# An attention kernel on one core: the first bias chunk is loaded behind q and k and added behind the scores

## The chip, the cores and the metric

The kernel runs on one core of one Trainium2 chip. The metric is device time in microseconds. Beside the times there is one profiled execution of the kernel before, with a trace of every instruction and of the DMA packets.

## The reference

Attention with a bias: 4 batches of 8 heads, 1024 positions, head dimension 64, all float32. The bias is one 1024 x 1024 matrix, shared by all heads.

```python
scale = 1.0 / np.sqrt(head_dim)
scores = scale * np.matmul(q, k.transpose(0, 1, 3, 2))
scores = scores + bias
scores_max = np.max(scores, axis=-1, keepdims=True)
attn = np.exp(scores - scores_max) / (np.sum(np.exp(scores - scores_max), axis=-1, keepdims=True) + 1e-8)
return np.matmul(attn, v).astype(np.float32)
```

## The kernel before

**Units of work.** The 32 heads form 16 pairs. The 1024 queries of a head form 8 chunks of 128 (query `p * 8 + c` is row `p` of chunk `c`). One slot is one head's chunk `c`: a 128 x 1024 block of scores, held transposed (keys down, queries across, in 8 pieces of 128 keys) in one of three places in PSUM (`places`, two banks each). A slot is filled by 8 score matmuls of 128 x 128 (L244), then ScalarE takes exp of it into a bfloat16 tile `E` (L258), and TensorE multiplies `E` with `v` and a column of ones (L312), so that the last column is the sum of the exps; VectorE divides (L320, L322) and SP stores. 19 of the 256 slots take their exp on VectorE by a polynomial instead.

**The bias is added once per place.** A run of slots in one place is made for the same chunk `c` and head after head. Only the first slot of a run (`start`, the fourth field in `slots`) gets the bias, by 8 matmuls of the bias with a scaled identity `ident8` (L241); the next slots add the difference of their scores and those of the head before to what lies in PSUM (the `ke`/`ko` and `qe`/`qo` arrays hold the pair's k and plus or minus q for that). The first three slots of the program are such starts: slot 0 is chunk 0 of head 0 in place 0, slot 1 chunk 1 in place 1, slot 2 chunk 2 in place 2. Each of the 8 bias matmuls of a slot takes every eighth column of the 1024 columns of `braw[:, c, :]`.

**Order of work.** The schedule is manual: the order in which the program issues instructions is the order on each engine. From slot 1's exp on it is made by a planner in the kernel, which keeps a model of the engines' times (`T0`, `bias_at`, `raw_at`, costs) and issues whatever its model has ready first. The planner's code and figures are the same in both kernels. What lies ahead of it, lines 335 to 392, is written out by hand, and that is what the change edits.

**The start, written out by hand.** Pair 0 is loaded in float32 by hardware queues: SP's queue takes `q0f` (the first `C0 = 3` chunks of q, 192 KB) and then `k0f` in two halves (256 KB each), ScalarE's queue takes `b0f`, bias chunk 0 (512 KB). GpSimd makes the identity, clears halves of `qz` and `qs` (two memsets, L350 and L351) and then issues the software loads, which cast to bfloat16 on the way: bias chunks 1 and 2, pair 1's k and q, pair 2's k and q, v of pair 0, and so on for the other pairs. TensorE meanwhile runs 10 matmuls of zeros (L360). Then: VectorE casts q and the first half of k (L370, L371); ScalarE casts the bias and then the second half of k (L372, L373); TensorE transposes q, k's first half and k's second half (L187, the last into PSUM place 2); VectorE copies them out to `qz`, `ko` and `qo` (L378, L199, L201). Slots 0 and 1 get their bias before their scores, and slot 0's exp is done in two halves, each as soon as half the keys' scores are there:

```python
for i in range(2):
    fill_half(0, i, "b")
transposes(0, 1, half, half, None, px=pk2)
copy_out(0, 1, half, half, pk2)
copy_out(0, 0, 0, C0, pq)
fill_half(0, 0, "s")
exp(0, 0, 1)
for i in range(2):
    fill_half(1, i, "b")
fill_half(0, 1, "s")
exp(0, 1, 1)
```

`fill(s)` then fills the rest of slot 1 (scores alone) and slot 2 (bias, then scores), and all slots after them.

Of the kernel before, what the change touches and what calls it, by code (L numbers as in the profile page):

```python
# [16 lines left out]
def kernel(  # L17
# [13 lines left out]
    nc = tc.nc  # L31
    B, H, S, D = q.shape
    P = 128
# [5 lines left out]
    qf = q.rearrange("b (g t) (p c) d -> (b g) p t (c d)", t=2, p=P)  # L39
    kf = k.rearrange("b (g t) (p c) d -> (b g) p t (c d)", t=2, p=P)  # L40
    vf = v.rearrange("b (g t) (p c) d -> (b g) p t c d", t=2, p=P)
    of = out.rearrange("b h (p c) d -> p (b h) c d", p=P)
    bf_ = bias.rearrange("a b (p c) k -> p (a b c) k", p=P)
# [9 lines left out]
    C0 = 3  # L53
# [22 lines left out]
    qs = consts.tile([P, NCH, P], BF)  # L76
    qz = [consts.tile([P, NCH, P], BF, name=f"qz{x}") for x in range(2)]
    zeros = ep.tile([P, NCH, P], BF, name="E")[:, :4].rearrange("p c q -> p (c q)")
    braw = consts.tile([P, NCH, S], BF)
# [4 lines left out]
    b0f = dp.tile([P, S], F32, name="df")  # L84
    q0f = dy.tile([P, S], I32, name="dy").bitcast(F32)[:, :2 * C0 * D].rearrange("p (t c d) -> p t c d", t=2, d=D)
    k0f = dp.tile([P, S], F32, name="dt").rearrange("p (t c d) -> p t c d", t=2, d=D)
    places = [ps_s.tile([P, 2, 512], F32, name=f"pl{x}") for x in range(3)]


    slots = []  # L90
# [72 lines left out]
    def load_v(pr):  # L163
        lands[pr, "v"] = vland.tile([P, 2, NCH, D], BF, name="v16")
        nc.gpsimd.dma_start(out=lands[pr, "v"].rearrange("p t c d -> p t (c d)"),  # L165
                            in_=vf[pr].rearrange("p t c d -> p t (c d)"))
        return lands[pr, "v"][:1, 1, NCH - 1, D - 1:]
# [14 lines left out]
    def transposes(pr, which, c0, n, tag, px=None):  # L182
        if px is None:
            px = ps_x.tile([P, n, P], BF, tag=tag, name="px")
        for c in range(n):
            if (pr, which, c0) in raws:
                nc.tensor.transpose(px[:, c, :], raws[pr, which, c0][:, c].rearrange("p t d -> p (t d)"), ident[:])  # L187
                continue

            for t in range(2):  # L190
                nc.tensor.transpose(px[t * D:(t + 1) * D, c, :], lands[pr, which, c0][:, t, c, :], ident[:],  # L191
                                    tile_position=(0, t * D))
        return px

    def copy_out(pr, which, c0, n, px):
        t = arrays(pr)
        cs = slice(c0, c0 + n)
        if which:
            nc.vector.tensor_copy(t["ko"][:, cs, :], px[:])  # L199
        else:  # L200
            nc.vector.tensor_scalar(t["qo"][:, cs, :], px[:], sgn[:], None, op0=ALU.mult)  # L201

    def double(pr, which, c0, n, part, w):

        t = arrays(pr)
        cs = slice(c0, c0 + n)
        rows = slice(D, P) if part == 1 else slice(0, D)
        to = arrays(pr + 1) if part == 1 else t
        if which:
            w.tensor_copy(to["ke"][rows, cs, :], t["ko"][rows, cs, :])  # L210
        else:
            w.tensor_scalar(to[("qe", "qe", "qs", "qz")[part]][rows, cs, :], t["qo"][rows, cs, :], -1.0, 1.0,
                            op0=ALU.mult, op1=ALU.mult)
# [11 lines left out]
    def operands(s):  # L225
        x, c, h, start = slots[s]
        pr = h // 2
        t = arrs[pr]
        if start:
            return t["ko"], t["qz"] if pr in first_pair else t["qs"]  # L230
        return (t["ko"], t["qo"]) if h % 2 else (t["ke"], t["qe"])

    def fill_half(s, b, what):

        x, c, h, start = slots[s]
        kk, qq = operands(s)
        for i in range(4):
            kc = 4 * b + i
            to = places[x][:, b, i * P:(i + 1) * P]
            if what == "b":  # L240
                nc.tensor.matmul(to, braw[:, c, :].rearrange("p (kp kc) -> p kc kp", kc=NCH)[:, kc, :], ident8[:],  # L241
                                 start=i == 0, stop=False, skip_group_check=True)
            else:
                nc.tensor.matmul(to, kk[:, kc, :], qq[:, c, :], start=False, stop=True, skip_group_check=True)  # L244

    def fill(s):
        for what in "bs" if slots[s][3] and s > 1 else "s":
            for b in range(2):
                fill_half(s, b, what)

    etile = {}

    def exp(s, i=0, n=2):

        if i == 0:
            etile[s] = ep.tile([P, NCH, P], BF, name="E")
        e = etile[s].rearrange("p (b c) q -> p b (c q)", b=2)
        nc.scalar.activation(e[:, i:i + n].rearrange("p b x -> p (b x)"),  # L258
                             places[slots[s][0]][:, i:i + n].rearrange("p b x -> p (b x)"), ACTF.Exp, scale=scale)
# [75 lines left out]
    with tc.manual_schedule():  # L335

        half = NCH // 2
        nc.sync.dma_start(out=q0f[:], in_=qf[0][:, :, :C0 * D].rearrange("p t (c d) -> p t c d", d=D))
        nc.scalar.dma_start(out=b0f[:], in_=bf_[:, 0, :])
        for i in range(2):  # L340
            nc.sync.dma_start(out=k0f[:, :, i * half:(i + 1) * half].rearrange("p t c d -> p t (c d)"),
                              in_=kf[0][:, :, i * half * D:(i + 1) * half * D])
        nc.vector.memset(zeros, 0.0)
        nc.vector.memset(warm[:], 0.0)
        nc.vector.memset(sgn[:D, :], -1.0)
# [2 lines left out]
        make_identity(nc, ident[:])  # L348

        nc.gpsimd.memset(qz[0][D:, :, :], 0.0)  # L350
        nc.gpsimd.memset(qs[D:, :, :], 0.0)  # L351
        for c in (1, 2):
            load_b(c)
        load_k(1)
# [1 line left out]
        load_k(2)  # L356
        load_q(2, slice(0, NCH))
        load_v(0)
        for i in range(10):
            nc.tensor.matmul(places[2][:, 0, :], zeros[:, :P], zeros, start=True, stop=True)  # L360

        cast = [de.tile([P, NCH, P], BF, name="de").rearrange("p c (t d) -> p c t d", d=D) for i in range(2)]
        qr0 = raws[0, 0, 0] = cast[0][:, half:half + C0]
# [5 lines left out]
        nc.vector.tensor_scalar(ident8[:], ident[:], 1.0 / scale, None, op0=ALU.mult)  # L369
        nc.vector.tensor_copy(qr0.rearrange("p c t d -> p t c d"), q0f[:])  # L370
        nc.vector.tensor_copy(kr0[0].rearrange("p c t d -> p t c d"), k0f[:, :, :half])  # L371
        nc.scalar.copy(braw[:, 0, :], b0f[:])  # L372
        nc.scalar.copy(kr0[1].rearrange("p c t d -> p t c d"), k0f[:, :, half:])  # L373

        pq = transposes(0, 0, 0, C0, "xa")
        pk = transposes(0, 1, 0, half, "xb")
        pk2 = places[2].bitcast(BF)[:, 1, :half * P].rearrange("p (c x) -> p c x", x=P)
        nc.vector.tensor_scalar(t0["qz"][:D, :C0, :], pq[:D], 1.0, None, op0=ALU.mult)  # L378
        copy_out(0, 1, 0, half, pk)
        for i in range(2):  # L380
            fill_half(0, i, "b")
        transposes(0, 1, half, half, None, px=pk2)
        copy_out(0, 1, half, half, pk2)
        copy_out(0, 0, 0, C0, pq)
        fill_half(0, 0, "s")
        exp(0, 0, 1)
        for i in range(2):
            fill_half(1, i, "b")
        fill_half(0, 1, "s")
        exp(0, 1, 1)  # L390
        double(0, 1, 0, NCH, 1, nc.vector)
        double(0, 0, 0, C0, 1, nc.vector)

# [363 lines left out]
        def dve_pick():  # L757

            can = [x for x in dve_q if (x[1] < 4 or len(dav) < 2) and (x[1] != 0.5 or len(open_d) < 3)]
            if not can:  # L760
                return None
            best = min(can, key=lambda x: (max(x[0], t_dve), x[1]))
            start = max(best[0], t_dve)

            if best[1] >= 3:
                soon = [x for x in can if x[1] < 3 and x[0] < start + 350]
                if soon:
                    best = min(soon, key=lambda x: (x[0], x[1]))
            return best
# [4 lines left out]
        while next_fill < NS or next_act < len(acts) or avq or dav or dve_q or sp_q:  # L774
            c = []
            if next_act < len(acts):

                s = min(x for x in acts[next_act:] if filled[x] <= max(t_act, filled[acts[next_act]]))
# [5 lines left out]
            d = dve_pick()  # L784
            if d:
                c.append((max(t_dve, d[0]), 1))
            p = pe_pick()
# [6 lines left out]
            if not c:  # L794
                p = min(pe_cands(), key=lambda x: x[0])
                c.append((p[0], 2))
            t, who = min(c)
            if who == 0:
                s = acts[next_act]
# [45 lines left out]
```

## Time and profile before

| | us |
|---|---|
| median of 3 runs (lowest, highest) | 233.12 (232.87, 233.36) |
| the profiled execution's own time | 233.77 |
| span of that profile, first to last instruction | 232.0 |
| PE busy in the span | 223.4 (96%) |
| ScalarE (ACT) busy | 221.5 (95%) |
| VectorE (DVE) busy | 196.8 (85%) |
| GpSimd (POOL) busy | 64.6 (28%) |

The difference of 1.8 us between the profiled execution's time and its span lies outside the instructions. In the lines of the profile, `L244 PE MATMUL pl<-qo,ko` is line, engine, operation and `out<-in` by the tiles' names. PE is the matmul side of TensorE and PEld its weight loads; SPq and ACTq are the DMA issues of SP and ScalarE. In the timeline, the first column is the start in the span and the second the duration, `xN` means that N instructions are merged into one line, and the bracket tells how long the engine was idle before it and what ended that. In the DMA view, q1 is SP's hardware queue, q10 ScalarE's, and q0 the software queue that GpSimd feeds. The granted clock of the profile is 1.00 in nearly the whole span.

### The profile page before, as it was taken

To read this page: it belongs to the slowest core of one execution; us is meant where nothing else is said; L and a number is where in the kernel's file an instruction comes from. 1 tells how busy PE (TensorE), PEld (TensorE's weight loads), DVE (VectorE), ACT (ScalarE), POOL (GpSimd) and SP (SyncE) were. 2 spreads that over 40 slices of the span, in tenths; PEclk is the share of its full clock that TensorE was granted. 3 is DMA by queue.
4 is the path that set the end of the run, shared out by engine and by line. 5 is a ranking of instruction groups with operands and counts; after the bars stand their busy time and mean duration, and the time that the engine had idled before them with its cause. 6 is when DMAs were issued, how large, how long until landed. Compare 5 with 4: busy or idle time off the path is not lost.

```text
span 232.0 us, 10693 instructions
## 1 busy us (share of the span) xinstructions
PE 223.4 (96%) x4671; PEld 210.0 (91%) x4671; DVE 196.8 (85%) x294; ACT 221.5 (95%) x242; POOL 64.6 (28%) x114
## 2 busy tenths in 40 slices
PE   7899999999999999999999999999999999999993
PEld 2779898899999999999999999999998999999992
DVE  2485768699988999799989789899999899999993
ACT  3699999999999999999999999999999999999994
POOL 8836653155553625325326210000000000000000
PEclk9999999999999999999999999999999999999999
DMA  6999999899999899998999965111111112112212
GB/s 200 210 205 225 215 226 223 185 114 120 168 189 142 126 192 151 123 173 155 191 206 197 237 114 128 43 37 40 42 37 49 39 48 57 54 29 71 68 38 62
DMA packets 55645, 29.75 MB, mean 128 GB/s; under 512 B 31856, under 2 KB 51952, under 8 KB 55600
## 3 DMA queue, kind: packets, MB, share of 16 engines
q0 software_dynamic: 30336, 14.06, 49.3%
q1 hardware_dynamic: 24832, 14.43, 22.4%
q8 instruction: 36, 0.59, 1.1%
q10 hardware_dynamic: 432, 0.59, 1.0%
q14 instruction: 9, 0.07, 0.1%
HBM read 29.36 MB, written 8.39 MB: 163 GB/s over the span
## 4 chain that ended last, share of the span: by engine, by line
ACT 25%; PE 15%; issue 11%; DMA 6%; DVE 6%; SPq 1%; DVEq 0%; ACTq 0%
ACT E L258 25%; PE pl L244 10%; PE po L312 4%; DMA out_dram<-ob 3%; DMA qe<-q 3%; SPq L694 1%; DVE ob L322 1%; DVE dt L290 1%; DVE dy L275 1%; DVE de L295 1%; PE px L191 1%; DVE df L280 1%; DVE df L287 0%; PE pl L241 0%; DVE rs L320 0%
## 5 line engine op out<-in xcount | busy, mean ns | idle before, releaser
L258 ACT ACTIVATE E<-pl 128x1024 bf16<-128x1024 f32 (+1 forms) x238 | 218.3, 1116 | 2.5 <-PE pl L244 2.1
L312 PE MATMUL po<-vall,E 128*128 128x65 bf16 x1896 | 92.0, 194 | 1.3 <-ACT E L258 0.7
L312 PEld LDWEIGHTS <-E 128*128 128x128 bf16 x1896 | 77.5, 98 | 2.4 <-ACT E L258 1.1
L244 PE MATMUL pl<-qo,ko 128*128 128x128 bf16 x1024 | 77.0, 219 | 1.0 <-ACT E L258 0.4
L244 PEld LDWEIGHTS <-ko 128*128 128x128 bf16 x1160 | 69.5, 98 | 4.1 <-issue 1.1
L244 PE MATMUL pl<-qe,ke 128*128 128x128 bf16 x888 | 66.3, 219 | 1.0 <-issue 0.3
L244 PEld LDWEIGHTS <-ke 128*128 128x128 bf16 x888 | 53.4, 98 | 3.9 <-issue 0.7
L275 DVE TENSOR_SCALAR dy<-pl 128x1024 int32<-128x1024 f32 x19 | 23.2, 1222 | 4.5 <-PE pl L244 3.7
L322 DVE TENSOR_TENSOR ob<-po,rs 128x448 f32<-128x448 f32 (+2 forms) x40 | 23.2, 581 | 3.4 <-DVE rs L320 1.1
L284 DVE SCALAR_TENSOR_TENSOR dt<-df 128x1024 f32<-128x1024 f32 x19 | 23.2, 1221 | 0.3
L295 DVE SCALAR_TENSOR_TENSOR de<-dy,dt 128x1024 uint16<-128x1024 int32 x19 | 23.2, 1219 | 0.1
L287 DVE SCALAR_TENSOR_TENSOR df<-dt,df 128x1024 f32<-128x1024 f32 x19 | 23.1, 1219 | 0.1
L290 DVE SCALAR_TENSOR_TENSOR dt<-df,dt 128x1024 f32<-128x1024 f32 x19 | 23.1, 1218 | 0.1
L138 POOL DMA_DIRECT2D q<-in_q_dram x18 | 16.7, 930 | 7.5 <-PE pl L244 6.1
L201 DVE TENSOR_SCALAR qo<-px,sgn 128x1024 bf16<-128x1024 bf16 (+2 forms) x18 | 12.4, 686 | 3.4 <-PE px L191 1.7
L199 DVE COPY ko<-px 128x1024 bf16<-128x1024 bf16 (+1 forms) x16 | 10.7, 671 | 4.4 <-PE px L191 4.0
L165 POOL DMA_DIRECT2D v<-in_v_dram x16 | 11.4, 712 | 10.1 <-DVE rs L320 6.5
L320 DVE RECIPROCAL rs<-po 128x7 f32<-128x7 f32 (+3 forms) x42 | 8.2, 195 | 6.3 <-PE po L312 6.0
L280 DVE TENSOR_SCALAR df<-dy 128x1024 f32<-128x1024 uint16 x19 | 13.2, 695 | 0.1
L241 PE MATMUL pl<-ident,braw 128*128 128x128 bf16 x136 | 11.5, 228 | 0.1
L468 POOL COPY tick<-q 1x1 bf16<-1x1 bf16 x13 | 4.2, 321 | 26.2 <-DMA q<-in_q_dram 25.9
L145 POOL DMA_DIRECT2D k<-in_k_dram x15 | 10.6, 710 | 2.3 <-issue 0.9
(55 smaller groups left out, 128.0 us busy)
## 6 DMA issues: line engine op xcount, KB each, us to landing
v<-in_v_dram POOLq DMA_DIRECT2D x16, 256.0 KB, 6.8
k<-in_k_dram POOLq DMA_DIRECT2D x15, 256.0 KB, 6.8
out_dram<-ob SPq DMA_DIRECT2D x35, 96.0 KB, 4.0
ke<-ko SPq DMA_DIRECT2D x22, 128.0 KB, 5.5
out_dram<-ob SPq DMA_DIRECT2D x40, 64.0 KB, 2.2
q<-in_q_dram POOLq DMA_DIRECT2D x18, 128.0 KB, 5.1
out_dram<-ob SPq DMA_DIRECT2D x68, 32.0 KB, 3.2
qe<-q SPq DMA_DIRECT2D x17, 128.0 KB, 5.4
```

The lines of the kernel that those rows point to most:

```text
L138: nc.gpsimd.dma_start(out=t[:, :, y, :], in_=(qf, kf)[x][pr][:, y].rearrange("p (c d) -> p c d", d=D))
L201: nc.vector.tensor_scalar(t["qo"][:, cs, :], px[:], sgn[:], None, op0=ALU.mult)
L244: nc.tensor.matmul(to, kk[:, kc, :], qq[:, c, :], start=False, stop=True, skip_group_check=True)
L258: nc.scalar.activation(e[:, i:i + n].rearrange("p b x -> p (b x)"), places[slots[s][0]][:, i:i + n].rearrange("p b x -> p (b x)"), ACTF.Ex ...
L275: w.tensor_scalar(t["y"][:], places[slots[s][0]].rearrange("p b x -> p (b x)"), scale * LOG2E * 65536.0, 127.0 * 65536.0, op0=ALU.mult, op ...
L280: w.tensor_scalar(t["f"][:], t["lo"], G / 65536.0, None, op0=ALU.mult)
L284: w.scalar_tensor_tensor(t["t"][:], t["f"][:], -G, t["f"][:], op0=ALU.add, op1=ALU.mult)
L287: w.scalar_tensor_tensor(t["f"][:], t["t"][:], Q, t["f"][:], op0=ALU.mult, op1=ALU.add)
L290: w.scalar_tensor_tensor(t["t"][:], t["f"][:], V, t["t"][:], op0=ALU.add, op1=ALU.mult)
L295: w.scalar_tensor_tensor(etile[s].bitcast(U16).rearrange("p c q -> p (c q)"), t["y"][:], 1.0 / 512.0, t["t"][:], op0=ALU.mult, op1=ALU.add)
L312: nc.tensor.matmul(po[:, j + i, :], etile[s][:, kc, :], vall[:, slots[s][2] % VR, kc, :], start=j + i + kc == 0, stop=kc == NCH - 1, skip_ ...
L322: nc.vector.tensor_tensor(ob[:, :n, :], po[:, :n, :D], rs[:, :n, :].to_broadcast([P, n, D]), op=ALU.mult)
```

## The change

Six edits, all ahead of the planner:

1. `b0f` is no longer loaded first on ScalarE's queue. The first half of `k0f` is loaded there, SP's queue takes `q0f`, the second half of `k0f`, and then `b0f` in two halves of 512 columns.
2. The `qs` memset moves on GpSimd from before the first software load to behind the seventh (behind `load_v(0)`).
3. TensorE's matmuls of zeros are 6 instead of 10 at first, and one more between the transposes of q and of k.
4. ScalarE casts the second half of k first and then the bias in two halves; the transposes of k's second half move ahead of VectorE's copies.
5. Slots 0, 1 and 2 get their scores first (with PSUM's start flag) and their bias behind them.
6. Slot 0's exp is one instruction over 1024 columns instead of two over 512.

```diff
-    def fill_half(s, b, what):
+    def fill_half(s, b, what, first):
...
             if what == "b":
                 nc.tensor.matmul(to, braw[:, c, :].rearrange("p (kp kc) -> p kc kp", kc=NCH)[:, kc, :], ident8[:],
-                                 start=i == 0, stop=False, skip_group_check=True)
+                                 start=first and i == 0, stop=not first, skip_group_check=True)
             else:
-                nc.tensor.matmul(to, kk[:, kc, :], qq[:, c, :], start=False, stop=True, skip_group_check=True)
+                nc.tensor.matmul(to, kk[:, kc, :], qq[:, c, :], start=first and i == 0, stop=not first, skip_group_check=True)
 
     def fill(s):
-        for what in "bs" if slots[s][3] and s > 1 else "s":
+
+        order = ("sb" if s < 3 else "bs") if slots[s][3] else "s"
+        for what in order:
             for b in range(2):
-                fill_half(s, b, what)
+                fill_half(s, b, what, len(order) > 1 and what == order[0])
...
-        nc.sync.dma_start(out=q0f[:], in_=qf[0][:, :, :C0 * D].rearrange("p t (c d) -> p t c d", d=D))
-        nc.scalar.dma_start(out=b0f[:], in_=bf_[:, 0, :])
+        for i, e in enumerate((nc.scalar, nc.sync)):
+            if i == 0:
+                nc.sync.dma_start(out=q0f[:], in_=qf[0][:, :, :C0 * D].rearrange("p t (c d) -> p t c d", d=D))
+            e.dma_start(out=k0f[:, :, i * half:(i + 1) * half].rearrange("p t c d -> p t (c d)"),
+                        in_=kf[0][:, :, i * half * D:(i + 1) * half * D])
+
         for i in range(2):
-            nc.sync.dma_start(out=k0f[:, :, i * half:(i + 1) * half].rearrange("p t c d -> p t (c d)"),
-                              in_=kf[0][:, :, i * half * D:(i + 1) * half * D])
+            nc.sync.dma_start(out=b0f[:, i * 512:(i + 1) * 512], in_=bf_[:, 0, i * 512:(i + 1) * 512])
...
-        nc.gpsimd.memset(qs[D:, :, :], 0.0)
...
         load_v(0)
-        for i in range(10):
-            nc.tensor.matmul(places[2][:, 0, :], zeros[:, :P], zeros, start=True, stop=True)
+        nc.gpsimd.memset(qs[D:, :, :], 0.0)
+
+        def keep_warm(n):
+            for i in range(n):
+                nc.tensor.matmul(places[2][:, 0, :], zeros[:, :P], zeros, start=True, stop=True)
+        keep_warm(6)
...
-        nc.scalar.copy(braw[:, 0, :], b0f[:])
         nc.scalar.copy(kr0[1].rearrange("p c t d -> p t c d"), k0f[:, :, half:])
+        for i in range(2):
+            nc.scalar.copy(braw[:, 0, i * 512:(i + 1) * 512], b0f[:, i * 512:(i + 1) * 512])
 
         pq = transposes(0, 0, 0, C0, "xa")
+        keep_warm(1)
         pk = transposes(0, 1, 0, half, "xb")
         pk2 = places[2].bitcast(BF)[:, 1, :half * P].rearrange("p (c x) -> p c x", x=P)
+        transposes(0, 1, half, half, None, px=pk2)
         nc.vector.tensor_scalar(t0["qz"][:D, :C0, :], pq[:D], 1.0, None, op0=ALU.mult)
         copy_out(0, 1, 0, half, pk)
-        for i in range(2):
-            fill_half(0, i, "b")
-        transposes(0, 1, half, half, None, px=pk2)
         copy_out(0, 1, half, half, pk2)
         copy_out(0, 0, 0, C0, pq)
-        fill_half(0, 0, "s")
-        exp(0, 0, 1)
         for i in range(2):
-            fill_half(1, i, "b")
-        fill_half(0, 1, "s")
-        exp(0, 1, 1)
+            fill_half(0, i, "s", True)
+        for i in range(2):
+            fill_half(0, i, "b", False)
+        exp(0)
```

## The prediction

> **What bounds the kernel now.** I read the ScalarE (ACT) rows after the start first: what does the engine with the least idle time wait for?
>
> ```profile
> L258 ACT ACTIVATE E<-pl 128x1024 bf16<-128x1024 f32 x236 | 217.3, 1120 | 1.3 <-PE pl L244 0.9 <-ACT E L258 0.3
> ```
>
> From slot 1's exp to the last one ACT works 217.3 us and idles 1.3 us: 236 exps, one after another. PE is about as full (223.4 us of the 232.0 us span by the page), but it is exps that follow without a break, and behind the last one there is only a tail of a few microseconds, which this change leaves alone. So the kernel is the start of slot 1's exp (10.00 us in the timeline), a block of 222 us, and whatever ACT starves in between. The change touches only what lies ahead of 10.00. The timeline shows how that time is made:
>
> ```profile
> 0.75 0.43 ACTq L339 DMA_DIRECT2D df<-in_bias_dram  x1
> 0.76 0.44 SPq L338 DMA_DIRECT2D dy<-in_q_dram  x1
> 1.20 4.45 PE L360 MATMUL pl<-E 128*128 128x512 bf16 x10 [1.20 <-DVE warm L344]
> 1.25 0.97 SPq L341 DMA_DIRECT2D dt<-in_k_dram  x2
> ...
> 3.17 1.24 POOL L160 DMA_DIRECT2D braw<-in_bias_dram  x2
> 5.43 1.04 ACT L372 CAST braw<-df 128x1024 bf16<-128x1024 f32 x1 [2.72 <-DMA df<-in_bias_dram]
> 5.69 0.36 DVE L370 CAST de<-dy 128x384 bf16<-128x384 f32 x1 [2.43 <-DMA dy<-in_q_dram]
> 6.48 0.43 DVE L371 CAST de<-dt 128x512 bf16<-128x512 f32 x1 [0.42 <-DMA dt<-in_k_dram]
> 7.11 0.62 ACT L373 CAST de<-dt 128x512 bf16<-128x512 f32 x1 [0.63 <-DMA dt<-in_k_dram]
> 7.20 0.66 PE L241 MATMUL pl<-ident,braw 128*128 128x128 bf16 x8
> ...
> 8.22 0.42 DVE L199 COPY ko<-pl 128x512 bf16<-128x512 bf16 x1 [0.39 <-PE pl L187]
> 8.44 0.60 ACT L258 ACTIVATE E<-pl 128x512 bf16<-128x512 f32 x1 [0.71 <-PE pl L244]
> 9.09 0.83 PE L244 MATMUL pl<-qz,ko 128*128 128x128 bf16 x12
> 9.51 7.01 ACT L258 ACTIVATE E<-pl 128x512 bf16<-128x512 f32 x8 [0.47 <-PE pl L244]
> ```
>
> The columns are start and duration. The bias (512 KB) is cast at 5.43, q at 5.69, k's halves at 6.48 and 7.11, each waiting for its transfer. The last chain is k's second half: cast 7.11 to 7.73, transposed, copied to `ko` (8.22 to 8.64), scores from 9.09, then the second half-exp at 9.51. From 10.00 ACT is fed: exps start 0.906 us apart (18.15 less 10.00, over nine).
>
> Third, the DMA view in two windows, since the change reorders transfers (packets, MB, share of 16 engines):
>
> ```profile
> q1 hardware_dynamic: 234, 0.23, 108.5%
> ```
>
> ```profile
> q0 software_dynamic: 79, 0.16, 80.5%
> q1 hardware_dynamic: 144, 0.13, 35.1%
> ```
>
> The first is 5.10 to 5.69: only SP's queue moves, 0.23 MB in 0.59 us, though GpSimd issued its first software load at 3.17. The second is 5.69 to 6.75: software packets come in as k's last packets leave.
>
> **The change, part by part.**
>
> *Order of the loads.* The same 1.25 MB (q 0.20, k and bias 0.52 each) are moved, as q, k, then bias. Before, the windows 1.8 to 3.9, 3.9 to 5.1 and 5.1 to 5.69 moved 0.46, 0.43 and 0.23 MB, and the last hardware packets ran until 6.75; k's cast followed at 7.11, so 0.35 us for a landing. At that pace q and k's first half (0.46 MB) are there by 3.9 + 0.35 = 4.25, k's second half (0.72 MB) by 4.65 + 0.35 = 5.0, against 5.69, 6.48 and 7.11. The bias is last. Its second half ends the same 1.25 MB and so lands at about 7.1; if the 0.39 MB/us of the first window held to the end it would be 6.35. I take 7.1, because the old 7.11 contains the same unevenness between the 16 DMA engines. `k0f`'s first half is issued where `b0f` was on ACT's queue (0.43 us, in front of the table load as before); SP issues four transfers instead of three, and its next work is the `ke` copy at 14.60: nothing waits there.
>
> *The score path.* q cast 4.25 to 4.61, k 4.6 to 5.04 (DVE rows 0.36 and 0.43), ACT's cast of the second half 5.0 to 5.62. Transposes, `qz` (0.34) and two copies (0.42 each) follow; from the first row of that chain to the end of the second copy it took 8.64 less 7.11 = 1.53 us, so `ko` is complete by some 6.6 and the eight score matmuls by 7.1. They are no longer last. The one `keep_warm` matmul between the transposes (0.43 us, a tenth of 4.45) lies inside this slack.
>
> *The bias path is what is last.* ACT casts the halves one after the other. One cast of 1024 columns took 1.04; 512 columns of k took 0.62. I take 0.6, with 0.52 and 0.62 as ends. The eight bias matmuls each read columns from both halves, so they start at 7.1 + 0.6 + 0.05 = 7.75, take 0.66 (L241), and the exp starts at 8.45. One exp of 1024 replaces two of 0.60: 0.91 in the cadence. It ends at 9.36. What the wait for the bias holds up on PE is slot 1's scores and all behind them; on ACT nothing but slot 0's exp. Slot 1 needs 8 score and 8 bias matmuls, 0.45 + 0.50 by the starts at 10.25, 10.70 and 9.75, issued behind slot 0's at 8.25: ready at 8.25 + 0.95 + 0.17 = 9.37, and its exp starts at 9.4, not 10.00. Slot 2, its order turned round too, needs 0.95 again against ACT's 0.906, so it is ready at 10.33 where its exp started at 10.91 before. **Gain 0.55 to 0.6 us** at the point from which ACT runs without a break; from slot 3 on both programs have the same order of work on every engine.
>
> *The software loads.* The `qs` memset (0.95 us, L351) goes behind seven load issues of some 0.7, so the first software load is issued at 2.27 instead of 3.17; the eighth, at 7.88 before, stays where it is. `qs` itself is needed only many pairs later. As the hardware transfers end no sooner, I give this edit nothing. Two loads bound the gain: chunk 2's bias lands at 3.85 + 5.7 = 9.5 and is wanted at 9.65 now; pair 1's k lands at 4.38 + 6.5 = 10.9 and was used at 11.24. And one wait shows already:
>
> ```profile
> 17.29 0.48 PEld L191 LDWEIGHTS <-k 128*64 128x64 bf16 x16 [0.29 <-DMA k<-in_k_dram]
> ```
>
> Pair 3's k ended a wait of 0.29 us. Shifted by 0.6, PE waits up to 0.9 there, but the fill behind it (17.86 to 18.48) is wanted by the exp at 19.05, then 18.45: just hidden. Above some 0.6 us the loads take back what the start gives.
>
> *Warm-up.* Three of ten idle-filling matmuls go. They never were on the path, but they run before the rest and the array's pace changes: 0.43 us for 512 columns in the warm-up, three transposes in 0.50, but 0.06 per 128 columns from 6.96 on. I count nothing, and price the other case below.
>
> *Sum.* The profiled execution took 233.77 us, its span 232.0 and 1.8 around it; 233.77 - 0.6 = 233.2. It lies 0.65 above the median of the three times shown, 233.12, so against that: **232.5 us**.
>
> **Rivals.**
>
> *The halves of the bias queue beside software loads (slower).* Before, k's second half was issued at 1.76 and the first software load 1.4 us later, and the two landings of k, 0.63 us apart for 0.26 MB, show no slowing. Now `b0f`'s second half is issued at about 2.27, in the same instant as the software load. Where a hardware transfer meets queued software loads it suffers: the `ke` copy of 128 KB issued at 14.60 took 5.2 us to land, while a 96 KB store at 164.0 took 1.6. Price: chunk 1's software load is 128 packets, 8 per DMA engine, at 0.16 us each (137 packets in 111.8% of 16 engines over 6.75 to 8): 1.3 us in front of the last half. Landing at 8.4 instead of 7.1 puts slot 1's exp at 10.7: 0.7 us slower, 233.8. It decides from a landing later than 7.7. The Trainium skill's page "DMA: Bandwidth & Descriptors" (Queues, rings and completion order) says an engine goes round between its queues packet by packet, which would give about this; the first window above, with no software packet for 2.5 us after the issue, does not look like it. 20%.
>
> *A slow array.* The warm-up ends at 1.20 + 6 x 0.43 = 3.77, and nothing runs until q's transposes at 4.65. If the quick pace is reached only by 9 or 10 us, the 16 matmuls of slots 0 and 1 take 0.107 (a quarter of 0.43) instead of 0.06 each: 8 bias matmuls cost 0.4 more, slot 1 0.75 more. Slot 1's exp then starts between 10.0 and 10.9: no change to 0.9 slower, say 233.4. The Trainium skill's page "TensorE: Matmul & The Clock Gate" (Part 1) has such a rule: half rate until about 3.4 us of activity, in a window that runs freely. By it the six matmuls, 2.6 us, need not be enough. For: the trace shows the step only after ten. Against: five groups of matmuls follow from 4.65 on. 15%.
>
> *The loads give it back (no change).* If pairs 1 to 3 land no sooner and PE's waits at them do starve ACT, or if the bias lands at 7.5, 0.1 to 0.3 us is left: 233.0. 17%.
>
> **How the numbers follow.** My forecast, 0.35 to 1.1 us gained (the upper end is a landing at 6.35 with the loads following), gets 48%. Over 0.2%, 0.47 us, is about what a measurement of this kernel can tell from no change. Most of the forecast lies beyond that, a little inside, so faster 0.45; the third rival, that part and the mild half of the slow array make 0.26; the first rival and the rest 0.29. The range runs from 232.0 (1.1 gained) to 233.9 (0.8 lost); the forecast's own is 232.0 to 232.8.
>
> **What would show it.** Right: casts of q and k at 4.3 to 5.0, the second bias cast near 7.1, slot 0's one exp near 8.45 and slot 1's near 9.4, and ACT's idle time behind it still about 1.3 us. Wrong: a second bias cast after 7.7 with software packets beside it, score matmuls 0.107 us apart after 7.5, or a PE wait of over 0.9 us for a k load at 10 to 18 us.

## The result, and the profile after

| | kernel before | changed kernel |
|---|---|---|
| median of 14 executions each, us (lowest, highest) | 233.24 (232.71, 235.14) | 234.46 (233.09, 236.98) |
| ratio, 95% interval | | 1.0051 [1.0026, 1.0076] |
| profiled execution, us (its span) | 233.77 (232.0) | 233.25 (231.5) |

The change makes the kernel half a per cent slower. The profiled execution does not show that: it is one of the shorter ones. Of the 26 executions of the changed kernel that were timed in two comparisons, 18 took over 234 us; of the 47 of the kernel before beside them, 5. (In all five comparisons it is 16 of 110 of the kernel before, 9 of them in a single comparison, so this share also differs between comparisons.) The loss lies in part of the executions, so it has to be found by experiments. But the one profile already shows where the start differs from the forecast. The timeline of its start, the changed kernel (start, duration; lines L367 to L389 are the hand-written start, L244 the scores, L241 the bias, L260 the exps):

```profile
2.27 1.24 POOL L160 DMA_DIRECT2D braw<-in_bias_dram  x2
4.52 0.87 DVE L378 CAST de<-dy 128x384 bf16<-128x384 f32 x1 [1.57 <-DMA dy<-in_q_dram]
5.32 0.56 DVE L379 CAST de<-dt 128x512 bf16<-128x512 f32 x1
5.62 0.62 ACT L380 CAST de<-dt 128x512 bf16<-128x512 f32 x1 [2.86 <-DMA dt<-in_k_dram]
6.25 1.20 ACT L382 CAST braw<-df 128x512 bf16<-128x512 f32 x2
...
7.32 1.03 PE L244 MATMUL pl<-qz,ko 128*128 128x128 bf16 x8
8.15 1.06 PE L241 MATMUL pl<-ident,braw 128*128 128x128 bf16 x8
9.00 0.66 PE L244 MATMUL pl<-qz,ko 128*128 128x128 bf16 x8
9.25 2.92 ACT L260 ACTIVATE E<-pl 128x1024 bf16<-128x1024 f32 x3 [1.79 <-PE pl L241]
```

q and k land 0.3 to 0.6 us later than forecast and the bias 0.3 sooner: its second half is cast by 7.45 (6.25 and two casts), where the forecast had 7.7. Then the array is slow: eight score matmuls take 1.03 us and eight bias matmuls 1.06, where eight take 0.66 from 9.00 on. So slot 0's exp starts at 9.25, not 8.45, and slot 1's at 10.20, not 9.4, which is 0.2 later than before. And yet this execution is no longer than one of the kernel before. ScalarE's group of all exps:

```profile
L260 ACT ACTIVATE E<-pl 128x1024 bf16<-128x1024 f32 x237 | 218.2, 1126 | 2.5 <-PE pl L241 1.8 <-PE pl L244 0.5
```

Of the 2.5 us of idle time 1.8 lie ahead of the first exp, so 0.7 behind it, where the line of before had 1.3: the block behind the start, which the prediction took as fixed, is shorter when it starts later.

The DMA view from 5.69 to 6.75, the second of the prediction's two windows, is almost as it was (q0 80 packets for 79, q1 76 for 144, since the bias's are twice as long as k's):

```profile
q0 software_dynamic: 80, 0.16, 83.2%
q1 hardware_dynamic: 76, 0.12, 30.2%
```

### The profile page after: what moved, and what is told of

It is laid out like the page before. It is cut to its first block, busy times and chain, and to the rows that moved or that the text cites. A ratio compares the mean times of both kernels' runs of the same rounds, so it can differ in the third digit from the quotient of the medians.

```text
span 231.5 us, 10689 instructions
## 1 busy us (share of the span) xinstructions
PE 222.7 (96%) x4668; PEld 210.6 (91%) x4668; DVE 196.9 (85%) x294; ACT 221.5 (96%) x242; POOL 65.9 (28%) x114
## 4 chain that ended last, share of the span: by engine, by line
PE 40%; ACT 35%; issue 15%; DVE 6%; DMA 2%; SPq 1%; DVEq 0%; ACTq 0%
ACT E L260 35%; PE pl L244 23%; PE po L314 11%; PE px L191 3%; PE pl L241 2%; DMA dy<-in_q_dram 2%; DVE ob L324 1%; PE px L187 1%; DVE dy L277 1%; SPq L701 1%; DVE df L282 1%; DVE dt L286 1%; DMA out_dram<-ob 1%; DVE dt L292 0%; DVE df L289 0%
## 5 line engine op out<-in xcount | busy, mean ns | idle before, releaser
L260 ACT ACTIVATE E<-pl 128x1024 bf16<-128x1024 f32 x237 | 218.2, 1126 | 2.5 <-PE pl L241 1.8
L244 PE MATMUL pl<-qo,ko 128*128 128x128 bf16 x1024 | 76.9, 219 | 1.1 <-ACT E L260 0.4
L244 PEld LDWEIGHTS <-ko 128*128 128x128 bf16 x1160 | 69.8, 98 | 4.5 <-issue 0.9
L244 PE MATMUL pl<-qe,ke 128*128 128x128 bf16 x888 | 66.2, 219 | 0.6
L244 PEld LDWEIGHTS <-ke 128*128 128x128 bf16 x888 | 53.5, 98 | 3.4 <-issue 0.2
L475 POOL COPY tick<-q 1x1 bf16<-1x1 bf16 x13 | 6.4, 489 | 24.9 <-DMA q<-in_q_dram 24.8
L241 PE MATMUL pl<-ident,braw 128*128 128x128 bf16 x136 | 11.9, 233 | 0.1
```

The costliest lines, as they stand in the source:

```text
L244: nc.tensor.matmul(to, kk[:, kc, :], qq[:, c, :], start=first and i == 0, stop=not first, skip_group_check=True)
```

## The experiments

**The two kernels once more.** The changed kernel as it is, timed again, and one more profiled execution of the kernel before.

> The changed kernel once more, unchanged, for a second trace and more times. Theory W (array's pace): TensorE starts at half pace and is let go to full pace only at the end of a 3.4 us window in which it was busy enough; with 6 warm-up matmuls whether and when that happens depends on where the windows fall. So the times spread again from about 233 to 237 us, and this trace shows the step from 0.107 to 0.056 us per matmul at another place than 9.1 us, or a fall back to half pace. Theory S (software loads): the earlier software loads hold up loads that are needed; then the start looks like that of the first trace and the loss shows as waits for DMA behind it.

> The kernel before once more, for a second trace. The first trace had its own late DMA engine (k's second half at 7.08). If late engines are chance, the half lands at 6.5 to 6.8 here, and slot 1's exp starts at 9.4 to 9.7 instead of 10.00.

Measured: 234.68 against 233.00 us, ratio 1.0065 [1.0034, 1.0096]; the single execution of the kernel before took 233.14. In this trace of the changed kernel TensorE is at full pace from 4.5 us on, and the start is what the prediction hoped for:

```profile
6.05 1.25 ACT L382 CAST braw<-df 128x512 bf16<-128x512 f32 x2
...
7.42 0.65 PE L241 MATMUL pl<-ident,braw 128*128 128x128 bf16 x8
...
8.11 5.66 ACT L260 ACTIVATE E<-pl 128x1024 bf16<-128x1024 f32 x6 [0.81 <-PE pl L241]
```

Slot 0's exp starts at 8.11 and slot 1's at 9.06, but the execution takes 233.21 us. In the second trace of the kernel before, k's second half is cast at 6.63 and not at 7.11, and slot 1's exp starts at 9.52, not 10.00. So 0.48 of the forecast 0.6 us was the lateness of the one trace that the sum was made from. This start still beats the second trace of before, by 0.46 us at slot 1's exp, and that was lost behind the start.

**Ten warm-up matmuls in the changed kernel.**

```diff
-        keep_warm(6)
+        keep_warm(10)
```

> The changed kernel with 10 warm-up matmuls ahead of q's transposes instead of 6 (they end at 1.20 + 10 x 0.427 = 5.47, where q's transposes started at 5.45). W: full pace by slot 0's scores in every run; slot 0's exp near 8.3, slot 1's near 9.3, 0.5 to 0.8 us faster than the kernel before (232.5) and a spread as narrow as its. S: nothing changes, 234 to 235 us as the changed kernel.

Measured: 234.15 us, 1.0049 [1.0017, 1.0081]. The pace is full from 4.1 us on, but now the bias is late in the trace:

```profile
6.32 0.62 ACT L382 CAST braw<-df 128x512 bf16<-128x512 f32 x1
8.18 0.62 ACT L382 CAST braw<-df 128x512 bf16<-128x512 f32 x1 [1.24 <-DMA df<-in_bias_dram]
```

By the DMA packets, a 2 KB packet of the bias's queue was held for 0.62 us at 5.1, and from 6.58 on the last five packets of the bias came only every 0.246 us, where they had come every 0.084. Software packets took 0.173 us each, so the spacing fits one of them between each two of the bias, on one DMA engine that had fallen behind; the records do not name the engine. That is the first rival's mechanism, with a landing of 8.16, beyond its 7.7. The time is about that of the changed kernel: restoring the warm-up alone gains nothing that can be seen.

**Six and one warm-up matmuls in the kernel before.**

```diff
-        for i in range(10):
-            nc.tensor.matmul(places[2][:, 0, :], zeros[:, :P], zeros, start=True, stop=True)
+        def keep_warm(n):
+            for i in range(n):
+                nc.tensor.matmul(places[2][:, 0, :], zeros[:, :P], zeros, start=True, stop=True)
+        keep_warm(6)
...
         pq = transposes(0, 0, 0, C0, "xa")
+        keep_warm(1)
```

> The kernel before with the changed kernel's warm-up alone: 6 matmuls and one more between the transposes of q and k. W: it loses as the changed kernel does, 0.5 to 2 us, with times spread over 3 us. S: as the kernel before, 233.2 us within 0.3.

Measured: 233.78 us, 1.0027 [1.0002, 1.0053]. In its trace the spacing of matmuls stays at 0.107 us until 10.0 (at full pace it is 0.056):

```profile
7.21 1.06 PE L241 MATMUL pl<-ident,braw 128*128 128x128 bf16 x8
...
8.92 1.06 PE L241 MATMUL pl<-ident,braw 128*128 128x128 bf16 x8
9.16 0.60 ACT L258 ACTIVATE E<-pl 128x512 bf16<-128x512 f32 x1 [1.82 <-PE pl L244]
```

The interval only just leaves out 1. Over all sixteen traces, those of the experiments below included: with ten matmuls (or 40 short ones) the full pace began between 4.1 and 7.1 us, in eleven traces; with six it began at 4.5, 4.6, 9.1, 10.0 and 10.6.

**Software loads at four times.** The `qs` memset back ahead of the software loads (the first issued at 3.17); that with ten warm-up matmuls, in two comparisons; that with the memset twice (first load at 4.16); and the changed kernel with the `qz` memset given to VectorE (first load at 1.44).

```diff
         nc.gpsimd.memset(qz[0][D:, :, :], 0.0)
+        nc.gpsimd.memset(qs[D:, :, :], 0.0)
...
         load_v(0)
-        nc.gpsimd.memset(qs[D:, :, :], 0.0)
```

> The changed kernel with the qs memset back ahead of the software loads. W: as the changed kernel, 234 to 235 us with a wide spread. S: most of the loss is gone, 233.2 us or less and a narrow spread.

> The changed kernel with the qs memset back ahead of the software loads and with 10 warm-up matmuls. Theory L (loads): the first software load, issued at 2.27 with the bias' second half, takes turns with it on any DMA engine that is late, 0.16 us for each of up to 16 packets, so that in a part of the executions the half lands 1 to 2.5 us late; issued at 3.17 it meets fewer of them. Theory W (pace): short warm-up leaves TensorE at half pace. If both hold, this is the best of the family: 232.6 to 233.2 us and a spread like that of the kernel before. If only L: 233.5 like the kernel with the memset alone. If only W: 234 and spread, like the one with the warm-up alone.

> The changed kernel with the qs memset ahead of the software loads and ten warm-up matmuls, once more, beside the two others. Theory 'both costs are mended and nothing is gained': 0.997 to 1.002, as before. Rival 'there is a gain which one comparison could not show': below 0.997. The profile of its first run was of a long execution (233.5 us of span), so a look at a shorter one is wanted: slot 1's exp near 9.1 and ScalarE's idle time up to 20 us under 1.5 us if the body is undisturbed; waits for the loads of k at 10 to 18 us if they take the start back.

> The kernel with the memset first and 10 warm-up matmuls, and the qs memset made twice, so that the first software load is issued at about 4.1 us. L: hardly any execution is left in which the bias' last half lands after 7.2 us; the spread is gone, but pair 1's loads land later, so that the median is 232.7 to 233.3. W alone: as the kernel with the warm-up alone, 234.1.

> The changed kernel with the memset of qz[0] made by VectorE, so that the first software load is issued at about 1.4 us instead of 2.27: the suspected cost made larger. L: the bias' halves land later in more executions, median 235 us or more. W alone: 234.5 as the changed kernel.

| first software load issued, us | warm-up matmuls | median us | ratio to the kernel before |
|---|---|---|---|
| 1.44 | 6 + 1 | 237.29 | 1.0158 [1.0114, 1.0202] |
| 2.27 (the change) | 6 + 1 | 234.46, 234.68 | 1.0051, 1.0065 |
| 2.27 | 10 + 1 | 234.15 | 1.0049 [1.0017, 1.0081] |
| 3.17 | 6 + 1 | 233.59 | 1.0030 [1.0010, 1.0050] |
| 3.17 | 10 + 1 | 233.61, 233.45 | 0.9995 [0.9969, 1.0022], 1.0005 [0.9987, 1.0023] |
| 4.16 | 10 + 1 | 234.66 | 1.0042 [1.0015, 1.0069] |

From 3.17 to 1.44, the sooner the loads, the worse (the intervals at 3.17 and 2.27 overlap, that at 1.44 stands clear); at 3.17 with the warm-up restored as well the loss is gone, which is what "both costs mended" means below. Later still is worse again: bias chunks 1 and 2 then land at 9.1 and 10.5, and slots 1 and 2 wait for them. With the loads at 1.44 the trace shows both costs at once (the second fence is the window view: busy time of PE, PEld, DVE, ACT, POOL, then the granted clock, DMA share and GB/s):

```profile
7.49 0.62 ACT L382 CAST braw<-df 128x512 bf16<-128x512 f32 x1 [1.52 <-DMA df<-in_bias_dram]
9.43 0.62 ACT L382 CAST braw<-df 128x512 bf16<-128x512 f32 x1 [1.32 <-DMA df<-in_bias_dram]
10.10 1.07 PE L241 MATMUL pl<-ident,braw 128*128 128x128 bf16 x8 [2.76 <-ACT braw L382]
```

```profile
4.64:8.05 3.41, 1.88 (x20) 1.18 (x20) 2.84 (x8) 1.18 (x2) 3.37 (x6) 1.00 1.11 271
8.05:14.88 6.83, 4.78 (x45) 4.78 (x46) 0.00 (x0) 2.98 (x5) 3.31 (x5) 0.50 1.25 210
14.88:20.00 5.12, 5.12 (x105) 4.34 (x103) 3.80 (x9) 5.12 (x6) 1.94 (x5) 1.00 1.24 205
```

In the DMA view from 5.10 to 5.69 of this run the two queues share the engines, where the prediction had found the hardware queue alone:

```profile
q0 software_dynamic: 42, 0.09, 76.6%
q1 hardware_dynamic: 36, 0.07, 36.6%
```

ScalarE waits 1.5 and 1.3 us for the bias, and TensorE 2.76 for its cast. Behind a stretch of 3.41 us in which TensorE was busy for 1.88, its granted clock is 0.50 for 6.83 us, so that eight matmuls take 1.07.

At 2.27 the effect is less plain. The first software packet of a run moved between 5.4 and 5.9 us in the four traces with the loads issued at 2.27, and between 5.5 and 5.8 in the ten with 3.17; at 1.44 it moved at 4.5. And the bias is late in one of the three traces of the changed order with 2.27 (the one with ten warm-ups), in none of the six with 3.17.

**The loads sooner in the kernel before, alone.** The same memset moved behind the seventh load, nothing else.

> The kernel before with one edit of the change alone: the qs memset goes behind the seventh software load, so that these are issued 0.9 us sooner (2.27 instead of 3.17). Nothing else of the change is in it: the bias is loaded first on ScalarE's queue, k last on SP's. Theory 'software packets take turns with the float32 loads that are last': the last float32 load is now k's second half, issued at 1.76, not the bias at 2.2 to 2.6, so there is less left for the software packets to meet, but k's second half has transposes, copies and scores behind it: its cast starts between 6.6 and 7.8, the ratio is 1.001 to 1.005, and more executions than one in ten are above 234. Rival 'the edit is harmless, or good by itself, because the bodies' loads land sooner': 0.998 to 1.000, as the prediction had it. Rival 'only the order with the bias last is hurt': 1.000.

Measured: 233.49 us, 1.0020 [0.9995, 1.0045]: unclear by itself. By the middle values, each good to some 0.0025, it makes 1.0047 with the short warm-up's 1.0027. That is about the change's 1.0051 and would leave some 1.000 for the new order of loads and sums.

**The bias on ScalarE's queue**, loads at 3.17 and ten warm-up matmuls.

```diff
-            nc.sync.dma_start(out=b0f[:, i * 512:(i + 1) * 512], ...)
+            nc.scalar.dma_start(out=b0f[:, i * 512:(i + 1) * 512], ...)
```

> The changed kernel with the qs memset ahead of the software loads again and ten warm-up matmuls, and with the two halves of the bias issued on ScalarE's queue behind k's first half (at some 1.25 and 1.7) instead of on SP's behind k's second half (1.75 and 2.2); ScalarE's table load moves back by 0.9 us, to some 2.2 to 3.5, where nothing waits for it. Theory 'what is left of the loss is in the loads of the body and not in the start': the start is as with SP's queue or 0.2 us sooner (second bias cast at 6.4 to 6.9, slot 0's exp at 7.9 to 8.4, slot 1's at 9.0), and the time is the same as the kernel before, ratio 0.998 to 1.001. Rival 'the bias is still late in part of the executions because its transfers are issued last': 0.995 to 0.998, and fewer executions above 234.

Measured: 233.33 us, 1.0004 [0.9986, 1.0021]; in its trace slot 1's exp starts at 9.48, hardly sooner than in the kernel before. Three comparisons with both costs mended thus give no gain, the two others although their traces start slot 1's exp at 9.13 and 9.17. Where does it go? From the traces, the starts of exps against the second trace of the kernel before, in us (exps counted on ScalarE, slot 0's halves as one):

| | slot 1 | 7th exp | 21st exp | 41st exp | last exp |
|---|---|---|---|---|---|
| kernel before, first trace | 0.48 | 0.47 | 0.47 | 0.57 | 0.60 |
| six warm-ups in the kernel before | 1.30 | 1.30 | 1.30 | 0.43 | 0.92 |
| changed kernel, first trace | 0.68 | 0.72 | 0.71 | 0.06 | 0.17 |
| changed kernel, second trace | -0.46 | -0.09 | -0.08 | 0.13 | 0.13 |
| ten warm-ups in the changed kernel | 1.03 | 1.17 | 1.18 | 0.88 | 0.86 |
| memset first | 1.04 | 1.16 | 1.16 | 0.39 | 0.36 |
| memset first, ten warm-ups (first) | -0.35 | 0.44 | 0.45 | 0.51 | 2.15 |
| memset first, ten warm-ups (second) | -0.39 | 0.36 | 0.36 | 0.16 | 0.36 |
| and the bias on ScalarE's queue | -0.04 | 0.04 | 0.06 | 0.15 | 0.14 |

The lead of an early start is gone by the seventh exp, near 14 us: in the three early starts here, and in the traces of "four loads" (-0.37, then 0.29) and "thirty more matmuls" (-0.43, then 0.80) below as well. There TensorE waits for the software loads of the next heads, most often for pair 1's k. The second trace of the kernel before comes to the transposes of that k at 10.76 without a wait:

```profile
10.76 0.48 PEld L191 LDWEIGHTS <-k 128*64 128x64 bf16 x16
```

The changed kernel's second trace, and the first one of "memset first, ten warm-ups", are there sooner and wait:

```profile
10.50 0.48 PEld L191 LDWEIGHTS <-k 128*64 128x64 bf16 x16 [0.26 <-DMA k<-in_k_dram]
...
13.31 1.07 PE L244 MATMUL pl<-qe,ke 128*128 128x128 bf16 x16 [0.21 <-DVE qe L212]
```

```profile
11.04 0.48 PEld L191 LDWEIGHTS <-k 128*64 128x64 bf16 x16 [0.61 <-DMA k<-in_k_dram]
```

VectorE's copies of this k and its q follow, and the scores of the seventh exp wait for them (13.31 above; 13.35 in the second trace of before). Pair 1's k landed between 10.3 and 11.1 us in all fifteen traces whose first software load was issued by 3.2 us, whether its own load was issued at 2.7, 3.5 or 4.4. So the loads did not move with the start.

A late start, on the other hand, loses part of its lateness further on. At slot 1 the table spreads over 1.8 us. At the 41st exp, near 46 us, it spreads over 0.9, the second trace of before being the 0.00, and over 0.6 without the row with ten warm-ups in the changed kernel. What evens it out? The PE timeline of the changed kernel's two traces has a stop that ends at nearly the same time in both, though one came 0.8 us later through the 21st exp (first trace, then second):

```profile
42.00 0.26 PE L314 MATMUL po<-vall,E 128*128 128x65 bf16 x3
42.49 0.59 PE L314 MATMUL po<-vall,E 128*128 128x65 bf16 x13 [0.24 <-issue]
```

```profile
41.73 0.26 PE L314 MATMUL po<-vall,E 128*128 128x65 bf16 x3
42.57 0.59 PE L314 MATMUL po<-vall,E 128*128 128x65 bf16 x13 [0.58 <-issue]
```

"issue" means that the profile shows no releaser. The stop is in the middle of a run of like matmuls, in all sixteen traces behind the 733rd recorded one and in six also behind the 606th, 127 earlier (254 rows with their weight loads). At the 733rd a 16 KB packet of the instruction queue q8 ends 1.3 to 1.5 us before TensorE goes on, every time. From the start of one matmul to the next, less the 0.056 us of a matmul, it costs 0.38 and 0.71 us in these two traces, the later one waiting less, and 0.68 in the second trace of the kernel before, which loses another 0.31 behind the 606th, where the changed kernel's first trace loses nothing. One experiment moves the instructions against the work.

**Thirty more matmuls ahead of the work.** The edit against memset first with ten warm-ups: 40 warm-up matmuls of 128 columns for the ten of 512.

```diff
-        keep_warm(10)
+        for i in range(40):
+            nc.tensor.matmul(places[2][:, 0, :P], zeros[:, :P], zeros[:, :P], start=True, stop=True)
```

> The changed kernel with the qs memset ahead of the software loads, and with 40 warm-up matmuls of 128 columns in place of ten of 512: the same 4.3 us of warm-up, but 30 more matmuls (with their weight loads) in TensorE's program ahead of all other work. Theory 'the wait is for a block of TensorE's code': it stays at the 606th and the 733rd matmul counted from the program's start, which are now 30 matmuls earlier in the work, so that TensorE comes to the latter near 40.5 to 41.0 instead of 41.8 and stands there for longer than 0.3 us, until some 1.4 us after an instruction packet's end. Rival 'it is at a place of the work' (a tile, a slot): it stays at the same instruction of the work, 30 matmuls later in the count.

```profile
34.75 0.29 PE L314 MATMUL po<-vall,E 128*128 128x65 bf16 x4
35.31 0.29 PE L314 MATMUL po<-vall,E 128*128 128x65 bf16 x4 [0.26 <-issue]
...
41.00 0.19 PE L314 MATMUL po<-vall,E 128*128 128x65 bf16 x1
41.55 0.39 PE L314 MATMUL po<-vall,E 128*128 128x65 bf16 x7 [0.36 <-issue]
```

The stops stay behind the 606th and the 733rd matmul from the program's start, now 30 matmuls earlier in the work, and the latter ends 1.36 us after its packet (40.19). So the stop belongs to the instructions and not to the work: TensorE waits for its own code there. The one execution of this version took 234.68 us.

**Fewer software loads in the queues**, in the version with both costs mended and in the kernel before.

```diff
-                nc.gpsimd.tensor_copy(tick[:], what)
+                nc.gpsimd.tensor_copy(tick[:], flight[-min(depth, 4)][0])
```

> The changed kernel with the qs memset ahead of the software loads and ten warm-up matmuls, and one more edit: GpSimd lets at most four instead of six software loads of its later list wait in the DMA queues (it waits for the fourth last before it issues the next); the planner's model, and with it the program of TensorE, VectorE and ScalarE, is unchanged. In every trace so far TensorE stands still for 0.15 to 1.0 us at the same matmul, the 733rd recorded one, near 42.5 us, and in most near the 606th, at 36; no engine releases it, and a 16 KB packet of the instruction queue ends 1.3 to 1.5 us before it goes on. Theory 'TensorE's own code comes behind the queued software loads, so a start gained is lost in that wait': with fewer loads queued the instruction packet starts some 2.5 us after the matmul 127 earlier instead of some 4, the waits at these two matmuls are under 0.2 us, slot 40's exp is as far ahead as slot 2's was, and the ratio is 0.996 to 0.999. Rival 'the loads themselves are the bound': with four in flight they land later, VectorE and TensorE wait for k and v, ratio 1.000 to 1.005. Rival 'the wait is not for code': it stays at that matmul with 0.4 us or more.

> The kernel before with that one edit alone (four instead of six loads of the later list in the queues). Theory 'TensorE's code comes behind the queued loads': the waits at the 606th and the 733rd matmul, 0.3 and 0.67 us in a trace of the kernel before, go, and the ratio is 0.996 to 0.999: by this the bound that ate the gain was there before the change. Rival 'the loads themselves are the bound': 1.000 to 1.005.

Measured: 235.71 us, 1.0102 [1.0078, 1.0125], and 234.40 us, 1.0054 [1.0040, 1.0067]: the rival held. The instruction packet did not come sooner (5.3 us after the 606th matmul in the former), the stop at the 733rd stayed at 0.99 and 0.66 us, and the loads fell behind. The DMA view from 10 to 40 us, the second trace of the kernel before and the mended version with four loads:

```profile
DMA packets 6568, 6.52 MB, mean 217 GB/s; under 512 B 581, under 2 KB 5983, under 8 KB 6561
```

```profile
DMA packets 6026, 5.97 MB, mean 199 GB/s; under 512 B 625, under 2 KB 5510, under 8 KB 6021
```

VectorE's wait for v between 9 and 44 us, in the same two kernels:

```profile
DVE vall L493 <- DMA v<-in_v_dram: 3.3, 4, 1.1
```

```profile
DVE vall L500 <- DMA v<-in_v_dram: 8.0, 6, 1.9
```

So slower loads make the whole kernel slower: until about 44 us the pace is set by transfers too, of data and of instructions, and not by the start alone. That faster ones would make it faster was not tried. Why the instruction packet starts some 4 us after the matmul 127 earlier is open too: thinning the software queue did not bring it sooner.

## Why the prediction was wrong

The forecast, 232.5 us, was a gain of 0.6; the result is a loss of 1.2 between the medians. Three steps failed, and each is a term that was set to nothing or taken as fixed.

*"As the hardware transfers end no sooner, I give this edit nothing"* (the software loads) is the first. Undoing this edit alone takes the ratio from 1.0051 and 1.0065 to 1.0030, some 0.5 to 0.8 us by the middle values (the intervals overlap), and bringing the loads forward once more costs another 2.2 to 2.5 us. The first rival had the mechanism, as the traces with the loads at 1.44 and with ten warm-ups show it; why issuing at 2.27 instead of 3.17 costs anything, when the first software packet moves no sooner, stays open. The rival's counter-evidence, a window in which no software packet moved, was no evidence: in the trace with ten warm-ups that window has one software packet beside 123 of the hardware queue, and the bias is late all the same, by its last five packets. The Trainium skill's page "DMA: Bandwidth & Descriptors" (Queues, rings and completion order) says that an engine goes round between its queues packet by packet; the trace with the loads at 1.44 agrees with such sharing in that very window (42 and 36 packets), and so does the spacing of 0.246 us in the one with ten warm-ups. In that window the hardware queue has the engines almost alone in the traces with the loads at 2.27 or 3.17; whether the software queue had work for them by then no view shows. The page's packet is several descriptors; whether a packet of these traces is one of those no run shows either.

*Warm-up, "I count nothing"* is the second. Alone on the kernel before, it costs 0.27% or 0.6 us (0.02 to 0.53%), and it is what the first trace of the changed kernel shows (1.03 and 1.06 us for eight matmuls, full pace from 9.1). The second rival had this too, at 233.4. Restored in the change alone it gave nothing to be seen (1.0049); only with the memset back in its place as well is the loss gone. The Trainium skill's page "TensorE: Matmul & The Clock Gate" (Part 1) has half rate until about 3.4 us of activity, in a window that runs freely; the granted clock's steps at 4.64, 8.05 and 14.88 us in the trace with the loads at 1.44 agree (3.41 and twice 3.41 apart). A free window would also explain why six matmuls sometimes sufficed (4.5) and mostly did not.

*"A block of 222 us"* behind slot 1's exp is the third, and it took the gain. The score and bias paths were right where the pace was full: in the second trace slot 0's exp starts at 8.11 and slot 1's at 9.06, sooner than the forecast 8.45 and 9.4. But of 0.46 us ahead at slot 1 0.09 were left at the seventh exp, and it was 0.13 us behind at the 41st. The prediction had the figures for the first of these losses: pair 1's k lands at 10.9 and was used at 11.24, so that 0.34 us of a gain fit, and 0.6 ask for it at 10.64. It named this bound and then added the whole 0.6. The third rival, pairs 1 to 3 landing no sooner, had the mechanism, and its price was nearest to what came of the kernels with both costs mended (ratios of 1.000). The place was not pair 3's k at 17 us, behind which no lead changes in the table's traces, but pair 1's k at 10.5 to 11.0 (in the trace of "thirty more matmuls" pair 2's, at 13.6), and later TensorE's own instructions. A late start can lose lateness there too: of 1.16 us 0.36 arrived at the end with the memset first, but 0.86 of 1.18 with ten warm-ups in the changed kernel.

The sum's base added to it: k's second half landed at 7.1 in the one trace of before, and at 6.6 in the next.

Right were the order of the landings (second bias cast at about 6.85 in the first trace, 7.1 forecast), the bias as the last thing on the path, and the one long exp in place of two.

What remains open is which of the two costs makes a given long execution, since no profile caught a long one of the changed kernel itself. Two profiles of other versions show a third kind: "memset first, ten warm-ups" (first trace) with a span of 233.5 us and the kernel before with sooner loads with 233.3. Both lost time far from the start, at the end of a block of instructions whose packet had come late; in the former:

```profile
119.37 0.44 PE L244 MATMUL pl<-qo,ko 128*128 128x128 bf16 x5
121.69 0.33 PE L244 MATMUL pl<-qo,ko 128*128 128x128 bf16 x3 [1.87 <-issue]
```

## What to carry to other kernels

A step that only moves a queue's first transfers is not free: ask which transfer is last on the path and whether another queue's packets can come between its own. Before a start is shortened, list the loads that the stretch behind it uses, with the time at which each lands and the time at which it will be wanted, and let the tightest of them bound the gain; compare two traces with different starts exp by exp, and see where the difference dies. Make the sum from more than one trace of the kernel before, and keep enough warm-up for every phase of the clock's window, not for the one seen.

## What the runs showed of the hardware

- TensorE's instructions come in 16 KB packets by DMA, one for 127 matmuls with their weight loads, and TensorE can run dry: 0.15 to 1.0 us (start to start, less one matmul) behind the 733rd matmul in all sixteen traces, between 41 and 46 us, and once 1.87 at 121.7 us. The Trainium skill's page "Runtime: NRT & Kernel Launch" (Instruction fetch mechanics) gives 16 KiB blocks of 256 instructions, which agrees, and calls the cost of crossing one mostly hidden, which these traces do not bear out while software loads fill the DMA engines.
- A software load that was issued sooner did not land sooner here: pair 1's k landed between 10.5 and 11.1 us in the four traces with the first load at 2.27, between 10.3 and 11.0 in the ten with 3.17, and at 10.6 with 1.44.
- VectorE's cast of q (128 x 384) took 0.36 us in ten traces and 0.47 to 0.62 in three, but 0.87, 1.03 and 0.77 in the three of the changed kernel with the loads at 2.27, where it ended at 5.4 however early it began; it stands beside GpSimd's load issues, but so it does where it took 0.36, and the cause was not tried.
- Now and then one 2 KB packet takes 0.4 to 1.3 us, in fourteen of the sixteen traces, where 0.084 to 0.096 (hardware queue) and 0.173 (software queue) are usual. With ten warm-ups in the changed kernel such a packet at 5.1 us went with a landing 1.5 us later than in the second trace of the changed kernel (8.16 against 6.66).
